# A hybrid decoder layer in float32: the mixer's sixteen group norms, one by one or four together

## The chip, the core and the metric

The kernel runs on one core of a Trainium2 chip. The metric is the device time of one execution in microseconds (us), the median of several runs. The engines are TensorE (PE, matmuls from SBUF into PSUM banks), VectorE (DVE), ScalarE (ACT), GpSimd (POOL) and SyncE (SP, which issues the loads). Each engine works through its own list of instructions in order, and waits where an operand is not there yet.

## What is computed

One layer over 1024 tokens of 1024 features, all in float32, cut to what matters here:

```python
u = rms_norm(x, norm1_g)
z = u @ w_in                      # 3 * 512 convolution columns, 4 * 512 retention columns
# convolution group: 512 features, 8 norm groups of 64
y_conv = cb * causal_dwconv3(cc * ch, conv_w)
y_conv = group_rms_norm(y_conv, conv_norm_g, 8)
# retention group: 4 heads of 128 features, one norm group each
o = chunkwise_retention(q, k, v)
y_ret = group_rms_norm(o, ret_norm_g, 4) * silu(rg)
x = x + concat([y_conv, y_ret]) @ w_out
x = x + relu(rms_norm(x, norm2_g) @ w_up)**2 @ w_down
return rms_norm(x, normf_g)

def group_rms_norm(x, g, n_groups, eps=1e-6):
    xg = x.reshape(shp[:-1] + (n_groups, shp[-1] // n_groups))
    y = xg * rsqrt(mean(xg * xg, axis=-1, keepdims=True) + eps)
    return y.reshape(shp) * g
```

## The kernel before

Features lie on the partitions, tokens on the columns. The unit of side work is a half tile, 128 features by 512 tokens. A float32 product is made of three matmuls of split operands, high by high, low by high and high by low: `wh` and `wl` are a weight's two parts, `uh` and `ul` those of the normed input, `yh` and `yl` those of the mixer's output. The high part is a cast (ACT), the low part a difference (DVE or POOL). Later tiles of the input projection are made in pairs by seven products of 2 x 2 blocks; their operands are `U`, made of `xs`, and each product's bank is combined with others by DVE (`z<-z,b`).

Up to the end of the mixer the products of the input projection fill PE, and everything else goes along with them: retention, convolution, the gate, the norms. That side work is written as generators (`Task`, `spawn`); each `yield` names the engines one of which is to do the next thing, or `None` for a thing that PE does. After each product `tick` calls `background` (line 390), which keeps an estimate of when each engine is through with what it has (`clock`) and of PE's time (`now`), and hands out steps to engines about to be idle. So the written order of every engine comes out of these estimates, and each engine then runs in that order.

The group norms are such generators. The mixer's output has eight tiles, four of the convolution (two norm groups of 64 features each) and four heads (one group of 128), and two halves of tokens: sixteen half tiles, each with a `norm` (line 433) of its own. It squares the half tile on ACT, splits the squares into a high part (ACT) and a low part (DVE or POOL), adds them up over the features of a group by two matmuls with a matrix of ones (`onesr`, or `blkr` with two blocks of 64; lines 445 and 446), which leaves the sum on every partition of a bank of its own; then comes a square root on ACT, a reciprocal on DVE over 128 partitions by 512 columns, and `done`, which scales: heads by `o<-o,r` on POOL or DVE, convolution tiles by `z<-z,sm,r` on DVE, which also multiplies by the norm's weight. At most two norms are open at a time (`asked`, `parts_of_s`). A scaled half tile is split into `yh` and `yl` for the output projection, whose first product takes eight k tiles in the order convolution 0 to 3, heads 0 to 3.

PSUM has eight banks, four for the large products (`pm`) and four for everything else (`pr`).

Of the kernel before, what the change touches and what calls it, by code (L numbers as in the profile page):

```python
# [16 lines left out]
P = 128  # L17
# [7 lines left out]
HB = 512  # hidden features in a block  # L25
# [6 lines left out]
# columns of the packed per-feature vectors  # L32
# [3 lines left out]
# tiles of w_in: 0-11 conv (c, h, b of each), 12-15 q, 16-19 k, 20-23 gate; two heads of q and k  # L36
# are a pair of tiles. The last ones go by pairs.
# [8 lines left out]
class Engine:  # L46
    """An engine, with a rough estimate of when it is through with what it has been given."""
# [23 lines left out]
def hybrid_layer(  # L71
# [12 lines left out]
    zeta: bass.AP,  # L84
    outT: bass.AP,
# [17 lines left out]
    # each engine runs its instructions in the order in which they are written here  # L103
# [24 lines left out]
    # ---- loads of the first phase  # L128
# [38 lines left out]
    plan, parts = [], []  # what makes the next pieces' parts, and the parts that are ready  # L167
# [19 lines left out]
    class Left:  # L187
        """The left operands of the products, for n_ pieces of each of the blocks."""
# [6 lines left out]
        def split(self, n, h=0):  # L195
# [29 lines left out]
    # ---- constants  # L225
    ones = cp.tile([P, 1], F32, name="ones")
    dve.memset(ones, 1.0)
    onesr = xp.tile([P, P], F32R, name="onesr")
    dve.tensor_copy(onesr, ones.to_broadcast([P, P]))
    eps = cp.tile([P, 1], F32, name="eps")  # L230
    dve.memset(eps, EPS)
    act.square(tmp()[:, :1], eps)  # loads the scalar engine's table while the first loads run
    onesf = xp.tile([P, P], F32, name="onesf")
    dve.memset(onesf, 1.0)
    blk = tmp()[:, :P]
    dve.memset(blk, 0.0)
    dve.memset(blk[0:64, 0:64], 1.0)
    dve.memset(blk[64:128, 64:128], 1.0)
    blkr = xp.tile([P, P], F32R, name="blkr")
    dve.tensor_copy(blkr, blk)  # L240
# [3 lines left out]
    def split_scaled(src, g, sl, hi, lo):  # L244
        """hi + lo = src * g, exactly, in two float32r parts."""
        act.activation(hi[:, sl], src[:, sl], AF.Copy, scale=g)
        dve.scalar_tensor_tensor(
            lo[:, sl], src[:, sl], g, f32(hi[:, sl]), ALU.mult, ALU.subtract
        )
# [10 lines left out]
    # ---- first norm's scale and sums  # L260
# [22 lines left out]
    nc.sync.dma_start(zxt, zeta)  # L283
    ropes = [unit(s="rope") for _ in range(6)]
# [3 lines left out]
    def token_rnorms(sums_, r, pool_=pr):  # L288
        """r = 1/sqrt(mean over features + eps), tokens on partitions."""
# [18 lines left out]
    def spread(wide, pool_=pr):  # L308
        """Reciprocal norms, tokens on partitions -> tokens on columns, on every partition."""
# [5 lines left out]
    # ---- v, tokens on partitions, and the tokens' reciprocal norms: on every partition in R,  # L315
    # with tokens on partitions in rtok
# [41 lines left out]

    def mm(piece, banks, rhs, start, stop, ks=range(4)):
        """Adds a piece's product with the parts of 4 tiles of [feature, token] into the banks."""  # L360
# [70 lines left out]
    asked, parts_of_s = [], [0]  # L431

    def norm(y, w, inv_n, done):
        """Norm over groups of features, the sums by a matrix of ones."""
        sq = tmp()
        sh = xp.tile([P, H], F32R, tag="s", name=nm("s"), bufs=4)
        yield (act,)
        act.square(sq, y)
        act.copy(sh, sq)
        eng = yield (dve, pool)  # L440
        slo = xp.tile([P, H], F32R, tag="s", name=nm("s"), bufs=4)
        eng.tensor_sub(slo, sq, f32(sh))
        yield None
        b = bank(pr)
        nc.tensor.matmul(b, w, sh, start=True, stop=False)
        nc.tensor.matmul(b, w, slo, start=False, stop=True)
        now[0] += 0.43
        parts_of_s[0] -= 1
        yield (act,)
        rt = xp.tile([P, H], F32, tag="s", name=nm("r"), bufs=4)  # L450
        act.activation(rt, b, AF.Sqrt, bias=eps, scale=inv_n)
        yield (dve,)
        dve.reciprocal(rt, rt)
        yield from done(rt)
        parts_of_s[0] -= 1

    def norms():
        while asked and parts_of_s[0] <= 2:
            parts_of_s[0] += 2
            y, w, inv_n, done, ready, late = asked.pop(0)  # L460
            spawn(norm(y, w, inv_n, done), ready, late)

    def tick(look=LOOK):
        n = -1
        while n != len(procs):
            n = len(procs)
            background(look)
            norms()

    def split_y_hi(idx, half):  # L470
        """Half a tile of the mixer's output in two parts."""
# [8 lines left out]
    def tile_in(evac):  # L480
        """A tile of the input projection, for both token halves."""
# [46 lines left out]
    def retention(p, q, k):  # L528
        """Step c finishes chunk c - 1 and starts chunk c."""
# [4 lines left out]
        for c in range(NC_ + 1):  # L534
# [30 lines left out]
            if pend is not None:  # L565
# [30 lines left out]
                if pc % 4 == 3:  # L596
                    half = pc // 4
                    for j in range(2):

                        def done(rt, j=j, half=half):  # L600
                            eng = yield (pool, dve)
                            eng.tensor_mul(o[j][:, hs[half]], o[j][:, hs[half]], rt)
                            o_n[h0 + j, half] = o[j]
                            mark(("o", h0 + j, half), eng)

                        asked.append((o[j][:, hs[half]], onesr, 1.0 / P, done, clock[act], 0.0))
# [32 lines left out]
    def conv_b(i, half, z, out, psum):  # L639
# [14 lines left out]
        asked.append((o, blkr, 1.0 / 64, done, clock[eng], LATE * half))  # L654
# [16 lines left out]
    def use(f, half, out, z, psum):  # L671
        """What a quadrant is for."""
# [30 lines left out]
    # ---- tiles of the convolution and of the gate: the first ones as they are, along with the  # L703
    # rest of the retention and the right operands of the seven products; then by pairs
# [25 lines left out]
    def rights(j):  # L730
        """The right operands of the seven products, for a tile of k in each half."""
# [107 lines left out]
    # ---- output projection and residual, by halves of the tokens; then the second norm's  # L839
# [537 lines left out]
```

## Time and profile before

| | |
|---|---|
| median of three runs | 1146.56 us |
| the three runs | 1143.61 to 1148.65 us |
| span of the profiled execution | 1146.0 us |
| mean granted clock of PE, share of full speed | 0.977 |
| PE busy | 1086.0 us, 95% |
| DVE busy | 895.8 us, 78% |
| POOL busy | 606.5 us, 53% |
| ACT busy | 496.3 us, 43% |

Busy is the time in which an engine executes; it says nothing of what the engine was waited for. Idle time of PE is listed with what ended it. Names are the program's, with buffer numbers left out: `z<-z,b` writes `z` from `z` and a bank. Line 65 is that of a helper through which DVE, ACT and POOL are called, so their instructions are told apart by names.

### The profile page before, as it was taken

What the parts mean: (1) busy time and instruction counts of PE and PEld (TensorE: products, weight loads), DVE (VectorE), ACT (ScalarE), POOL (GpSimd) and SP (SyncE); (2) the same over time, 40 slices, a digit from 0 to 9 for tenths busy, and PEclk for the clock granted to TensorE, in tenths of its full rate; (3) what the DMA queues carried; (4) which work ended last, traced back from release to release, by engine and by line L of the source; (5) the groups of instructions that cost most, each with busy time, mean ns of one, the idle gap of its engine ahead of it and who ended that gap; (6) DMA issues with size and microseconds to landing.
All of it is one profiled execution on the core that took longest, in us unless ns stands there. A gap on an engine that the chain in (4) does not pass through costs nothing.

```text
span 1146.0 us, 13780 instructions
## 1 busy us (share of the span) xinstructions
PE 1086.0 (95%) x4880; PEld 887.1 (77%) x4880; DVE 895.8 (78%) x1118; ACT 496.3 (43%) x906; POOL 606.5 (53%) x413
## 2 busy tenths in 40 slices
PE   8999999998798999779999999999999999999897
PEld 6888888886676788657788788787887887887686
DVE  8795686699999647798878788788887887887745
ACT  8212431555344545345444434443434444344553
POOL 6363234457576214877636637437355366374353
PEclk9999999999899999889999999999999999999998
DMA  7311112221112742010120130121211201200104
GB/s 258 138 55 55 28 37 83 79 88 37 37 37 65 274 131 82 0 46 28 56 83 19 55 84 25 58 65 39 73 37 55 83 19 55 83 26 13 55 19 148
DMA packets 40309, 77.73 MB, mean 68 GB/s; under 512 B 4528, under 2 KB 6576, under 8 KB 40240
## 3 DMA queue, kind: packets, MB, share of 16 engines
q1 hardware_dynamic: 40240, 76.85, 21.1%
q8 instruction: 38, 0.62, 0.2%
q14 instruction: 31, 0.25, 0.1%
HBM read 72.64 MB, written 4.19 MB: 67 GB/s over the span
## 4 chain that ended last, share of the span: by engine, by line
PE 50%; DVE 29%; issue 8%; POOL 7%; ACT 5%; DMA 0%; DVEq 0%; POOLq 0%; SPq 0%; ACTq 0%
PE b L365 34%; PE b L1130 8%; DVE wl L65 8%; DVE x L65 7%; PE b L327 4%; POOL t L65 4%; DVE t L65 3%; DVE V L65 2%; ACT wh L65 2%; DVE U L65 2%; ACT t L65 2%; POOL r L65 2%; DVE r L65 1%; DVE z L65 1%; DVE un L65 1%
## 5 line engine op out<-in xcount | busy, mean ns | idle before, releaser
L65 DVE TENSOR_TENSOR wl<-r,wh 128x512 fp32r<-128x512 f32 x273 | 250.4, 924 | 141.1 <-ACT wh L65 140.6
L365 PE MATMUL b<-U,wh 128*128 128x512 f32 x992 | 316.4, 399 | 12.7 <-DVE U L65 8.4
L65 ACT CAST wh<-r 128x512 fp32r<-128x512 f32 x302 | 181.1, 615 | 173.5 <-PE b L365 116.3
L1130 PE MATMUL b<-V,wh 128*128 128x512 f32 x784 | 245.0, 392 | 11.5 <-POOL V L65 10.6
L65 POOL TENSOR_TENSOR r<-r,r 128x512 f32<-128x512 f32 x136 | 205.3, 1515 | 76.9 <-DVE wl L65 36.7
L365 PEld LDWEIGHTS b<-U,wh 128*128 128x128 f32 x992 | 189.9, 192 | 59.5 <-DVE U L65 13.1
L65 DVE TENSOR_TENSOR x<-x,b 128x512 f32<-128x512 f32 (+1 forms) x320 | 197.9, 664 | 11.4 <-PE b L365 11.4
L365 PE MATMUL b<-U,wl 128*128 128x512 f32 x496 | 197.5, 398 | 0.4 <-DVE wl L65 0.4
L65 ACT ACTIVATE t<-t 128x512 f32<-128x512 f32 x128 | 80.8, 632 | 243.3 <-DVE t L65 241.1
L1130 PEld LDWEIGHTS b<-V,wh 128*128 128x128 f32 x784 | 147.7, 188 | 45.6 <-POOL V L65 13.6
L65 POOL TENSOR_TENSOR t<-t,t 128x512 f32<-128x512 f32 x69 | 101.1, 1485 | 124.3 <-ACT t L65 61.9
L1130 PE MATMUL b<-V,wl 128*128 128x512 f32 x392 | 154.4, 394 | 2.4 <-DVE wl L65 2.4
L365 PEld LDWEIGHTS b<-U,wl 128*128 128x128 f32 x496 | 95.0, 192 | 24.2 <-DVE wl L65 4.4
L365 PE MATMUL b<-uh,wh 128*128 128x512 f32 x320 | 107.3, 400 | 4.3 <-DVE z L65 4.3
L65 POOL TENSOR_TENSOR V<-t,V 128x512 fp32r<-128x512 f32 x35 | 51.1, 1459 | 105.1 <-ACT V L65 105.1
L365 PE MATMUL b<-ul,wh 128*128 128x512 f32 x320 | 106.0, 396 | 0.7 <-DVE ul L65 0.7
L365 PE MATMUL b<-uh,wl 128*128 128x512 f32 x320 | 105.6, 395 | 0.0
L65 POOL TENSOR_TENSOR wl<-r,wh 128x512 fp32r<-128x512 f32 x29 | 39.3, 1357 | 98.6 <-ACT wh L65 92.8
L1130 PEld LDWEIGHTS b<-V,wl 128*128 128x128 f32 x392 | 73.8, 188 | 21.3 <-DVE wl L65 6.2
L65 ACT CAST V<-t 128x512 fp32r<-128x512 f32 x98 | 60.4, 617 | 42.9 <-POOL t L65 42.9
L65 DVE TENSOR_TENSOR t<-t,b 128x512 f32<-128x512 f32 x112 | 75.9, 678 | 2.6 <-PE b L365 1.0
L365 PEld LDWEIGHTS b<-uh,wh 128*128 128x128 f32 x320 | 60.2, 191 | 17.5 <-issue 4.4
(157 smaller groups left out, 1511.9 us busy)
## 6 DMA issues: line engine op xcount, KB each, us to landing
r<-w_up_t SPq DMA_DIRECT2D x64, 256.0 KB, 2.6
r<-w_down_t SPq DMA_DIRECT2D x56, 256.0 KB, 2.6
r<-w_in_t SPq DMA_DIRECT2D x48, 256.0 KB, 2.6
r<-w_out_t SPq DMA_DIRECT2D x32, 256.0 KB, 2.7
xt<-xT SPq DMA_DIRECT2D x16, 256.0 KB, 5.4
xs<-xT SPq DMA_DIRECT2D x8, 512.0 KB, 6.2
x<-xT SPq DMA_DIRECT2D x8, 512.0 KB, 7.8
rope<-rope SPq DMA_DIRECT2D x6, 512.0 KB, 7.2
```

The source lines that it names most:

```text
L65: return f(out, *args, **kw)
L327: nc.tensor.matmul(vb[i], a[k][:, tsl], b[k // 2][:, vs], start=(k == 0 and a is uh and b is vh), stop=(k == KT - 1 and a is ul),)
L365: nc.tensor.matmul(b, a[:, k, :], rhs(n, k)[r], start=(start and i == 0), stop=(stop and i == len(ops) - 1),)
L1130: nc.tensor.matmul(b, a, r, start=(i == 0), stop=(i == len(ops) - 1))
```

## The change

The norms go by batches of four half tiles: two heads by two halves, or two convolution tiles by two halves. `ask` collects them; `norms` replaces `norm`.

- Squares and their two parts are made as before. The matmuls that add up the parts now have a selection matrix on the left that has ones in two columns only, so half tile s's sums go to rows 2s and 2s + 1 of one bank that the whole batch shares, and again to rows 32 + 2s and 33 + 2s.
- One square root and one reciprocal over that bank serve the four.
- The result is split: ACT casts it, DVE replaces rows 32 to 63 of the cast by the low part (32x512).
- Each half tile gets its factor back on all partitions by one spread matmul with another selection matrix, into a bank. `done` reads the bank; heads are now scaled by DVE only.
- The selection matrices (128x780) are loaded from DRAM ahead of the rope tables and cast once by ACT; `onesr`, `blkr` and what made them are gone. At most two open norms is no longer a rule.

The rest of the diff takes comments away. Its core:

```diff
+BATCH = 4
+NSELECT = BATCH * P + 2 * (P + 2 * (BATCH - 1))
...
+    sel_raw = unit(s="selw")[:, :NSELECT]
+    nc.sync.dma_start(sel_raw, select)
...
+    sel = unit(F32R, "sel")[:, :NSELECT]
+    act.copy(sel, sel_raw)
...
-    def norm(y, w, inv_n, done):
-        """Norm over groups of features, the sums by a matrix of ones."""
-        sq = tmp()
-        sh = xp.tile([P, H], F32R, tag="s", name=nm("s"), bufs=4)
-        yield (act,)
-        act.square(sq, y)
-        act.copy(sh, sq)
-        eng = yield (dve, pool)
-        slo = xp.tile([P, H], F32R, tag="s", name=nm("s"), bufs=4)
-        eng.tensor_sub(slo, sq, f32(sh))
-        yield None
-        b = bank(pr)
-        nc.tensor.matmul(b, w, sh, start=True, stop=False)
-        nc.tensor.matmul(b, w, slo, start=False, stop=True)
...
+    def norms(kind, items):
+        inv_n = (1.0 / 64, 1.0 / P)[kind]
+        b = None
+        for s, (y, _) in enumerate(items):
+            sq = tmp()
+            sh = xp.tile([P, H], F32R, tag="s", name=nm("s"), bufs=4)
+            yield (act,)
+            act.square(sq, y)
+            act.copy(sh, sq)
+            eng = yield (dve, pool)
+            slo = xp.tile([P, H], F32R, tag="s", name=nm("s"), bufs=4)
+            eng.tensor_sub(slo, sq, f32(sh))
+            yield None
+            if b is None:
+                b = bank(pr)
+            nc.tensor.matmul(b, gather(kind, s), sh, start=(s == 0), stop=False)
+            nc.tensor.matmul(b, gather(kind, s), slo, start=False, stop=(s == len(items) - 1))
+            now[0] += 0.45
         yield (act,)
         rt = xp.tile([P, H], F32, tag="s", name=nm("r"), bufs=4)
         act.activation(rt, b, AF.Sqrt, bias=eps, scale=inv_n)
+        del b
         yield (dve,)
         dve.reciprocal(rt, rt)
-        yield from done(rt)
-        parts_of_s[0] -= 1
...
+        yield (act,)
+        rows = xp.tile([P, H], F32R, tag="s", name=nm("s"), bufs=4)
+        act.copy(rows, rt)
+        yield (dve,)
+        dve.tensor_sub(rows[32:64], rt[32:64], f32(rows[32:64]))
+        for s, (_, done) in enumerate(items):
+            yield None
+            rb = bank(pr)
+            nc.tensor.matmul(rb, place(s), rows, start=True, stop=True)
+            now[0] += 0.23
+            yield from done(rb)
+            del rb
...
                         def done(rt, j=j, half=half):
-                            eng = yield (pool, dve)
-                            eng.tensor_mul(o[j][:, hs[half]], o[j][:, hs[half]], rt)
+                            yield (dve,)
+                            dve.tensor_mul(o[j][:, hs[half]], o[j][:, hs[half]], rt)
```

On DVE, around the last two reciprocals of the convolution tiles before (`z_2428` is tile 3, `r` the factor, `b` a product's bank):

```order
L65 TENSOR_TENSOR z_2599<-z_2599,b_2706 128x512
L65 RECIPROCAL r_2727<-r_2727 128x512
L65 TENSOR_TENSOR z_2600<-z_2600,b_2731 128x512
L65 TENSOR_TENSOR z_2600<-z_2600,b_2653 128x512
L65 TENSOR_TENSOR wl_2773<-r_2595,wh_2772 128x512
L65 TENSOR_TENSOR z_2600<-z_2600,b_2759 128x512
L65 SCALAR_TENSOR_TENSOR z_2428<-z_2428,sm,r_2727 128x512
L65 RECIPROCAL r_2756<-r_2756 128x512
L65 TENSOR_TENSOR wl_2820<-r_2670,wh_2819 128x512
L65 SCALAR_TENSOR_TENSOR z_2428<-z_2428,sm,r_2756 128x512
```

and around the last one after the change, that of tiles 2 and 3 together (`s_2865` holds the rows that the spread matmuls read):

```order
L69 RECIPROCAL r_2835<-r_2835 128x512
L69 TENSOR_TENSOR z_2753<-z_2753,b_2843 128x512
L69 TENSOR_TENSOR z_2752<-z_2753,b_2783 128x512
L69 TENSOR_TENSOR wl_2884<-r_2771,wh_2883 128x512
L69 TENSOR_TENSOR z_2753<-z_2753,b_2868 128x512
L69 TENSOR_TENSOR z_2753<-z_2753,b_2783 128x512
L69 TENSOR_TENSOR s_2865<-r_2835,s_2865 32x512
L69 TENSOR_TENSOR wl_2907<-r_2800,wh_2906 128x512
L69 TENSOR_TENSOR z_2753<-z_2753,b_2891 128x512
```

Two reciprocals with a scaling behind each have become one reciprocal and a 32x512 difference; the scalings stand further on, in the next place.

On PE and on DVE at the end of the mixer. Before, on PE, the last product of the input projection (`uh`, `ul`) is followed by the first output product (`yh_2827` is tile 0):

```order
L365 MATMUL b_2947<-ul_161,wh_2849 128x512
L365 MATMUL b_2947<-uh_153,wl_2850 128x512
L365 MATMUL b_3001<-yh_2827,wh_2884 128x512
L365 MATMUL b_3001<-yl_2828,wh_2884 128x512
L365 MATMUL b_3001<-yh_2827,wl_2885 128x512
L365 MATMUL b_3001<-yh_2831,wh_2884 128x512
```

After, the four spreads stand between them:

```order
L379 MATMUL b_2918<-ul_153,wh_2826 128x512
L379 MATMUL b_2918<-uh_145,wl_2827 128x512
L481 MATMUL b_2938<-s_2865,sel_539 128x512
L481 MATMUL b_2955<-s_2865,sel_539 128x512
L481 MATMUL b_2958<-s_2865,sel_539 128x512
L481 MATMUL b_2961<-s_2865,sel_539 128x512
L379 MATMUL b_2993<-yh_2802,wh_2858 128x512
L379 MATMUL b_2993<-yl_2803,wh_2858 128x512
L379 MATMUL b_2993<-yh_2802,wl_2859 128x512
```

and on DVE, behind the emptying of the last product's bank (the first row), come the scalings of tiles 2 (`z_2199`) and 3 (`z_2392`), in between the gate's products (`o`) and low parts (`yl`):

```order
L69 TENSOR_TENSOR z_2752<-z_2752,b_2918 128x512
L69 SCALAR_TENSOR_TENSOR z_2199<-z_2199,sm,b_2938 128x512
L69 SCALAR_TENSOR_TENSOR o_1568<-z_2753,sm,o_1568 128x512
L69 TENSOR_TENSOR yl_2944<-z_2199,yh_2943 128x512
L69 TENSOR_TENSOR yl_2949<-o_1568,yh_2948 128x512
L69 SCALAR_TENSOR_TENSOR o_1567<-z_2752,sm,o_1567 128x512
L69 SCALAR_TENSOR_TENSOR z_2199<-z_2199,sm,b_2955 128x512
L69 SCALAR_TENSOR_TENSOR z_2392<-z_2392,sm,b_2958 128x512
L69 SCALAR_TENSOR_TENSOR z_2392<-z_2392,sm,b_2961 128x512
L69 TENSOR_TENSOR yl_2965<-z_2392,yh_2964 128x512
```

where before there were these, without any scaling of a convolution tile:

```order
L65 TENSOR_TENSOR z_2782<-z_2782,b_2947 128x512
L65 SCALAR_TENSOR_TENSOR o_1600<-z_2783,sm,o_1600 128x512
L65 TENSOR_TENSOR z_2782<-z_2782,R 128x512
L65 TENSOR_TENSOR yl_2970<-o_1600,yh_2969 128x512
L65 SCALAR_TENSOR_TENSOR o_1599<-z_2782,sm,o_1599 128x512
```

On ACT, the square root of the last batch with what stands behind it (`s_2865` is the cast that waits for DVE's reciprocal, `wh` are casts of weights):

```order
L69 ACT_TABLE_LOAD
L69 ACTIVATE r_2835<-b_2667,eps 128x512
L69 CAST yh_2838<-o_838 128x512
L69 CAST wh_2858<-r_2747 128x512
L69 ACT_TABLE_LOAD
L69 ACTIVATE z_2752<-z_2752 128x512
L69 CAST s_2865<-r_2835 128x512
L69 CAST wh_2883<-r_2771 128x512
L69 CAST wh_2906<-r_2800 128x512
```

Before, no cast of a norm's factor stood among the casts of weights.

## Rows read from the trace of the kernel before

**Rows 1.** The page: busy time of each engine, share of the span, instructions.

```profile
PE 1086.0 (95%) x4880; PEld 887.1 (77%) x4880; DVE 895.8 (78%) x1118; ACT 496.3 (43%) x906; POOL 606.5 (53%) x413
```

**Rows 2.** Windows: stretch, length, busy us (instructions) of PE, PEld, DVE, ACT, POOL; clock.

```profile
60.00:120.00 60.00, 60.00 (x294) 50.65 (x293) 39.67 (x43) 10.77 (x26) 25.74 (x15) 1.00 0.17 53
120.00:240.00 120.00, 120.00 (x635) 102.78 (x634) 87.51 (x102) 45.15 (x101) 45.35 (x33) 1.00 0.22 73
240.40:377.00 136.60, 119.38 (x479) 94.38 (x478) 132.31 (x121) 65.30 (x104) 91.35 (x59) 0.94 0.16 47
377.00:460.00 83.00, 83.00 (x370) 68.79 (x369) 47.74 (x65) 42.31 (x73) 28.09 (x20) 0.98 0.45 155
```

**Rows 3.** Waits of PE from 240 to 380 us: total, times, longest.

```profile
PE b L365 <- DVE z L65: 7.7, 4, 3.6
...
PE b L446 <- POOL s L65: 3.0, 1, 3.0
PE b L446 <- DVE s L65: 2.2, 1, 2.2
```

**Rows 4.** DVE's groups, 240.4 to 377 us: busy, mean ns | idle before.

```profile
L65 DVE RECIPROCAL r<-r 128x512 f32<-128x512 f32 x8 | 26.7, 3342 | 0.7 <-ACT r L65 0.7
L65 DVE TENSOR_TENSOR wl<-r,wh 128x512 fp32r<-128x512 f32 x21 | 21.8, 1038 | 0.2
L65 DVE TENSOR_TENSOR z<-z,b 128x512 f32<-128x512 f32 x28 | 18.9, 674 | 2.7 <-PE b L365 1.9 <-DVE z L65 0.5
...
L65 DVE SCALAR_TENSOR_TENSOR z<-z,sm,r 128x512 f32<-128x512 f32 x6 | 8.0, 1326 | 0.0
...
L65 DVE TENSOR_TENSOR s<-t,s 128x512 fp32r<-128x512 f32 x5 | 6.2, 1238 | 0.0
```

**Rows 5.** Timeline of DVE: start us, duration us, instruction.

```profile
279.13 1.77 DVE L65 TENSOR_TENSOR wl<-r,wh 128x512 fp32r<-128x512 f32 x1
...
294.86 3.34 DVE L65 RECIPROCAL r<-r 128x512 f32<-128x512 f32 x1
...
299.38 0.68 DVE L65 TENSOR_TENSOR wl<-r,wh 128x512 fp32r<-128x512 f32 x1
...
301.19 0.74 DVE L65 SCALAR_TENSOR_TENSOR z<-z,sm,r 128x512 f32<-128x512 f32 x1
```

**Rows 6.** Timeline of PE: start us, duration us, instruction, idle before it.

```profile
298.89 0.77 PE L365 MATMUL b<-uh,wh 128*128 128x512 f32 x1 [3.59 <-DVE z L65]
...
304.15 0.63 PE L365 MATMUL b<-uh,wh 128*128 128x512 f32 x1
304.57 0.47 PE L365 MATMUL b<-ul,wh 128*128 128x512 f32 x1
...
366.31 0.39 PE L365 MATMUL b<-yh,wh 128*128 128x512 f32 x1
366.54 0.39 PE L365 MATMUL b<-yl,wh 128*128 128x512 f32 x1
...
374.40 0.50 PE L365 MATMUL b<-yh,wh 128*128 128x512 f32 x1 [3.17 <-ACT yh L65]
```

**Rows 7.** Windows of 10 us, columns as in rows 2.

```profile
290.00:300.00 10.00, 5.74 (x23) 4.10 (x22) 9.93 (x9) 2.87 (x5) 7.22 (x5) 0.90 0.00 0
300.00:310.00 10.00, 10.00 (x36) 7.96 (x35) 8.03 (x11) 3.81 (x6) 2.98 (x2) 0.76 0.29 80
```

**Rows 8.** Chain that ended last, 240 to 380 us: shares, then start and length.

```profile
by line: PE b L365 30.1%; DVE r L65 9.6%; DVE z L65 9.5%; DVE wl L65 9.0%; DVE xs L65 8.7%; issue 7.9%; DVE cv L65 5.8%; DVE ul L65 4.1%; DVE o L65 4.0%; DVE U L65 3.9%; ACT xs L65 2.8%; DVE yl L65 1.0%; ACT wh L65 0.9%; PE b L446 0.8%; DVE
...
294.94 3.26 DVE r L65
...
298.89 8.24 PE b L365 x23
```

More of the change, by code (lines that the diff above doesn't have):

```diff
@@ L84, in hybrid_layer @@
     zeta: bass.AP,
+    select: bass.AP,
     outT: bass.AP,
@@ L227, in hybrid_layer @@
     dve.memset(ones, 1.0)
-    onesr = xp.tile([P, P], F32R, name="onesr")
-    dve.tensor_copy(onesr, ones.to_broadcast([P, P]))
     eps = cp.tile([P, 1], F32, name="eps")
@@ L234, in hybrid_layer @@
     dve.memset(onesf, 1.0)
[L235 to L240, printed above, removed]
     ident = cp.tile([P, P], F32, name="ident")
@@ L357, in hybrid_layer, with gather, place @@
     prepare(2)
+    sel = unit(F32R, "sel")[:, :NSELECT]
+    act.copy(sel, sel_raw)
+    del sel_raw
+    STRIP = P + 2 * (BATCH - 1)
+    def gather(kind, s):
+        at = BATCH * P + kind * STRIP + 2 * (BATCH - 1 - s)
+        return sel[:, at : at + P]
+    def place(s):
+        return sel[:, s * P : (s + 1) * P]
     def mm(piece, banks, rhs, start, stop, ks=range(4)):
@@ L430, in hybrid_layer @@
     y, y_h, y_l = [None] * KT, [None] * KT, [None] * KT
-    asked, parts_of_s = [], [0]
-    def norm(y, w, inv_n, done):
-        sq = tmp()
-        sh = xp.tile([P, H], F32R, tag="s", name=nm("s"), bufs=4)
-        yield (act,)
-        act.square(sq, y)
-        act.copy(sh, sq)
-        eng = yield (dve, pool)
-        slo = xp.tile([P, H], F32R, tag="s", name=nm("s"), bufs=4)
-        eng.tensor_sub(slo, sq, f32(sh))
-        yield None
-        b = bank(pr)
-        nc.tensor.matmul(b, w, sh, start=True, stop=False)
-        nc.tensor.matmul(b, w, slo, start=False, stop=True)
-        now[0] += 0.43
-        parts_of_s[0] -= 1
+    asked = {}
+    def norms(kind, items):
[16 more added lines that the diff above has]
+            now[0] += 0.45
         yield (act,)
@@ L451, in norm, with ask @@
         act.activation(rt, b, AF.Sqrt, bias=eps, scale=inv_n)
+        del b
         yield (dve,)
         dve.reciprocal(rt, rt)
-        yield from done(rt)
[L455 to L461, printed above, removed]
+        yield (act,)
[10 more added lines that the diff above has]
+            del rb
+    def ask(key, kind, y, done, ready):
+        items = asked.setdefault(key, [])
+        items.append((y, done, ready))
+        if len(items) == BATCH:
+            del asked[key]
+            spawn(norms(kind, [i[:2] for i in items]), max(i[2] for i in items))
     def tick(look=LOOK):
@@ L467, in tick @@
             background(look)
-            norms()
     def split_y_hi(idx, half):
@@ L600, in done @@
                         def done(rt, j=j, half=half):
-                            eng = yield (pool, dve)
-                            eng.tensor_mul(o[j][:, hs[half]], o[j][:, hs[half]], rt)
+                            yield (dve,)
+                            dve.tensor_mul(o[j][:, hs[half]], o[j][:, hs[half]], rt)
                             o_n[h0 + j, half] = o[j]
-                            mark(("o", h0 + j, half), eng)
-                        asked.append((o[j][:, hs[half]], onesr, 1.0 / P, done, clock[act], 0.0))
+                            mark(("o", h0 + j, half), dve)
+                        ask(("heads", p), 1, o[j][:, hs[half]], done, clock[act])
             pend = new
@@ L652, in done @@
             mark(("y", i, half), dve)
-        asked.append((o, blkr, 1.0 / 64, done, clock[eng], LATE * half))
+        ask(("conv", i // 2), 0, o, done, clock[eng])
     def gate(h, half, z, g, psum):
@@ L1300, in _constants @@
     zeta = np.exp(lg[None, :] * (P - 1.0 - i)[:, None]) * scale
-    return [np.ascontiguousarray(a, np.float32) for a in (rope, decay, zeta)]
+    place = np.zeros((P, BATCH, P))
+    strips = np.zeros((P, 2, P + 2 * (BATCH - 1)))
+    c = 2 * (BATCH - 1)
+    for at in (0, 32):
+        for g in range(2):
+            for s in range(BATCH):
+                place[at + 2 * s + g, s, g * 64 : (g + 1) * 64] = 1.0
+            strips[g * 64 : (g + 1) * 64, 0, at + c + g] = 1.0
+            strips[:, 1, at + c + g] = 1.0
+    select = np.concatenate([place.reshape(P, -1), strips.reshape(P, -1)], axis=1)
+    return [np.ascontiguousarray(a, np.float32) for a in (rope, decay, zeta, select)]
 def kernel(x, norm1_g, w_in, conv_w, conv_norm_g, ret_norm_g, w_out, norm2_g, w_up, w_down,
@@ L1346 @@
     )
-    rope, decay, zeta = _constants()
+    rope, decay, zeta, select = _constants()
     arrays = {
@@ L1362 @@
         "zeta": zeta,
+        "select": select,
     }
```

## The prediction

> **What bounds the kernel now.** The table of engines comes first: TensorE (PE) is busy 95% of the span and VectorE (DVE) 78% [rows 1]. Neither is the answer everywhere, so the second view cuts the span where the changed work lies. The kernel up to the end of the mixer has 16 group norms. From 120 to 240 us PE has no idle time at all, from 377 to 460 us again none; between, from 240.4 us (the second convolution tile's product leaves its bank) to 377.0 us (the first output tile is added to x), DVE is busy 132.3 of 136.6 us and PE 119.4 [rows 2]. There DVE is the bound, and there eight of the sixteen norms' reciprocals run.
>
> The third view says who PE waits for in that stretch: 7.7 us for DVE's combining of two banks (`z`), 5.3 us at two sum matmuls for the low part `s` of the squares, made by POOL and by DVE [rows 3]; most of the rest of PE's 17 us is the 3.17 us at 374.40 for a head's `yh` [rows 6]. The fourth groups DVE's instructions: a reciprocal takes 3.34 us, five times a two-operand instruction's 0.67 [rows 4]. The timeline shows one acting: from 294.86 to 298.12 us DVE is in a reciprocal, the bank that PE needs is emptied behind it, and PE, after 3.59 us of idling, goes on at 298.89 [rows 5, 6, 8]. Until 304.57 it issues a matmul each 0.427 us, at full clock each 0.227 us [rows 6]; the granted clock of that slice and the next is 0.90 and 0.76, a mixture of 2.4 and 1.2 GHz [rows 7]. The chain of work that ended last takes both pieces in, the reciprocal and the slow products [rows 8].
>
> **The change, part by part.**
>
> *Reciprocals and square roots.* The instruction order has four reciprocals where there were sixteen, in the bound stretch three where there were eight: 5 x 3.34 = 16.7 us of DVE saved. The twelve square roots less lie on ACT, busy 65 of 136.6 us [rows 2]: nothing.
>
> *What DVE gets for it.* In the stretch the order shows DVE with 120 instructions before and 133 after. Gone besides the reciprocals: six `z<-z,sm,r`, two `wl`, one `xs` difference. New: eight `z<-z,sm,b` (the factor now read from PSUM), four `o<-o,b` (two were POOL's, two belonged to heads scaled earlier), three low parts of 32x512, four `s`, two each of `z<-z,R`, `z<-z,cv` and `yl`, two sums of squares: 27. No row shows `z<-z,sm,b`; it is bounded below by `z<-z,b`, one operand in PSUM, 0.674 us, and above by `z<-z,sm,r`, 1.326 us in the mean and 0.74 us alone [rows 4, 5]; I take 0.72, because the operand from PSUM is what it has in common with the first and the scalar with the second. The 32x512 low part is bounded by 0.68 and 1.77 us, the same operation on 128 partitions alone and with POOL beside it [rows 5]. With every instruction at its price alone: gone 16.7 + 6 x 0.74 + 3 x 0.68 = 23.2; new 8 x 0.72 + 19 x 0.68 = 18.7; net -4.5 us.
>
> *How much of it is lengthening.* A `wl` took 1.77 us at 279.13, while POOL ran, and 0.68 us at 299.38 [rows 5]. Reciprocals and the instructions that read a bank are never lengthened (3.342 and 0.674 in the mean [rows 4]). So 8 x 3.34 + 33 x 0.67 = 48.8 us of the stretch are cover under which POOL costs DVE nothing; the other 80 instructions take 132.3 - 48.8 = 83.5 us, 29 us more than 80 x 0.68. With 59 POOL instructions in the stretch [rows 2] that is 0.49 us each, or 0.77 for each that falls outside the cover (48.8 of 136.6, 36%). After the change POOL has 51 there by the order (`o<-o,r`, some `s` and `z<-z,cv` go to DVE), and the cover is 3 x 3.34 + 45 x 0.67 = 40 us, 31% of some 130. 51 x 0.77 x 0.69 = 27 us: another -1.9. DVE's term is **-6.4 us**. Ends: if every added instruction costs its group's mean (1.238 for `s`, 0.674 for what reads a bank [rows 4]), the sum shrinks to about -2.5; if the lengthening goes with POOL's instructions alone, at 0.49 each, it is -4.5 - 3.9 = -8.4.
>
> The rule that speaks against this edit is in the Trainium skill, "SBUF — State Buffer", section "Who interferes with whom": a DVE instruction with two SBUF inputs contends with a GpSimd instruction that reads SBUF, one with at most one SBUF input does not. The trace agrees (1.77 against 0.68 us; the reciprocal always 3.34), so the change takes away DVE instructions of the kind that does not contend. By it DVE's term is the -6.4 above; without it the -8.4, and the time 1138.6.
> A second one, "VectorE: DVE Perf Modes", section "The TRN2 errata", gives a VectorE instruction with PSUM 62 cycles more than one with SBUF alone; by it the twelve that now read PSUM would cost an estimated 0.8 us more, 1141.4 in all. The rows differ: 0.674 with a bank, 0.68 without [rows 4, 5].
>
> *PE's waits and clock.* The clock's part of the stall behind the reciprocal at 294.86 us lies on the chain: 13 matmuls at 0.427 instead of 0.227 us are **-2.6 us** if that stall goes [rows 6, 8]. The wait itself is DVE's time and is in DVE's term. What is late next there is the next emptying, since DVE stays full.
>
> *Matmuls.* 32 sum matmuls become 32 gathers and 16 spreads. Ahead of 240 us there are four fewer, at 0.227 us on a full PE [rows 2, 6]: **-0.9 us**. In the stretch there are twenty more, 4.5 us, under PE's 17 us of idling: nothing, unless DVE ceases to bind.
>
> *New places where PE waits.* Gathers and spreads stand in PE's order at some 23 places of the stretch instead of 7. Of the seven, two waited, 5.3 us together [rows 3]; but in the chain of waits second sum matmuls (line 446) hold only 0.8% of the 140 us from 240 to 380, 1.1 us [rows 8]. At 1.1/7 each sixteen more cost 2.5 us, at 5.3/7 each 12 us. I take half of the lower, **+1.2 us**, since what they wait for is made by engines that have less to do.
>
> *The end of the mixer.* The second convolution batch is finished last. Its four spreads stand directly ahead of the first output product, and the scaling of tiles 2 and 3 behind the last emptying on DVE. The output product needs tile 3 as the fourth of eight k tiles: 15 of its 24 matmuls follow what comes last, before it was 3 (three `yh`/`yl` sets of head 3 at 374.40 us [rows 6]). 12 x 0.227 = **+2.7 us**. The scalings themselves are in DVE's term.
>
> *Small parts.* The selection matrix's load stands ahead of the rope loads on SP's queue and its cast on ACT ahead of the first products; PE is full from 60 to 240 us [rows 2], so a rope tile that comes a microsecond later is hidden by products; uncovered it would be that microsecond. Constants dropped at the start ran while DVE waited for loads: nothing. The MLP's instructions are in the same order on every engine.
>
> Sum: -6.4 - 2.6 - 0.9 + 1.2 + 2.7 = -6.0 us. The profiled execution spans 1146.0 us; the median of the three times is 1146.56, so the sum is put against the median: **1140.6 us**.
>
> **Rivals.**
> *PE becomes the bound.* If DVE is relieved so that PE seldom waits, the stretch is PE's: 479 + 20 matmuls x 0.227 = 113 us, plus the end's wait of 3 and some 5 for half clock and gaps, 121.5 instead of 136.6: 1131 us. For it: DVE's waits are nearly all of PE's. Against: DVE alone has 132 us there and loses a few only.
> *No gain.* The work swapped for reciprocals is two-operand work at its mean price: -2.5, the tail +2.7, places +2.5, the rest -0.9 and the clock's 2.6 not given back: about +2: 1146 to 1148. For it: `s` at 1.24 and `wl` at 1.04 in the mean; against: eight POOL instructions less.
> *Slower: ACT held behind the batch.* The cast of the reciprocal's rows stands in ACT's order ahead of casts of weights (`wh`) and waits for the reciprocal on DVE, which waits for four half tiles' sums. In the written order weights are cast two to three products ahead, each product 12 x 0.227 = 2.7 us, so 5 to 8 us of lateness are covered. Beyond that PE stops: each batch then costs a stall like the 3.59 us and the 2.6 us of half clock behind it, three batches 18.6 us, against the 6 gained: 1159 us; with one or two batches 1147 to 1153. It decides from the point where the reciprocal starts more than 8 us after the square root. For it: DVE has no slack; against: ACT is half idle.
> That the change would not do what it says, the order excludes: the reciprocals are gone.
>
> **How the numbers follow.** The sum, with DVE's ends and the places' doubled, runs from 1136 to 1145, chance 0.45, and a little over half of that lies beyond 0.5% faster. PE the bound: 0.18. No gain: 0.25. ACT held: 0.12. Half a per cent, 5.7 us, is about what a measurement of this kernel can tell from no change; the bounds are 1140.8 and 1152.3. Faster: 0.26 + 0.18 and a little of the no-gain case, 0.46; same 0.43; slower 0.11. The range leaves out half of the slower case and the outer part of PE's: 1131 to 1150.
>
> **What would show it.** In the changed trace: three reciprocals between the second convolution tile's product and the first output tile; that stretch at 130 to 131 us with DVE still 95% busy or more; POOL's lengthening of two-operand instructions unchanged; a granted clock above 0.94 in it; a PE wait at the first output product on tile 2 or 3 rather than on head 3; `z<-z,sm,b` at 0.70 to 0.75 us. DVE below 93% with PE full would make the first rival right; ACT idle ahead of a cast `s<-r` with PE waiting for `wh` or `wl`, the third; a stretch of 136 us with two-operand instructions at 1.1 us and more, the second. A stall of PE of over 3 us at the four spreads would make the end's term wrong.

## The result

The changed kernel takes 1149.28 us in the median of 14 runs, beside 1146.28 us of the kernel before on the same chip: a ratio of 1.0027, 95% interval 1.0015 to 1.0040, 3 us slower. Two repeats of it on other chips gave 1.0041 (1.0026 to 1.0056) and 1.0036 (1.0023 to 1.0050). The forecast was 1140.6 us, so the range of 1131 to 1150 holds the time, but the sign is wrong: it went the other way, by half of what was forecast.

The page of the changed kernel shows what was meant to happen. DVE's busy time fell by 35.5 us, POOL's by 23 [rows 1]:

```profile
span 1147.5 us, 13774 instructions
## 1 busy us (share of the span) xinstructions
PE 1085.9 (95%) x4896; PEld 884.5 (77%) x4896; DVE 860.3 (75%) x1119; ACT 490.6 (43%) x899; POOL 583.1 (51%) x399
```

Where the time went is read by cutting both profiles at the same events: the second convolution tile's product (where the stretch of [rows 2] begins), the last product of the input projection, the first output tile's addition `x<-x,b`, and the eighth. First the kernel before, then the change (stretch, length, busy us and instructions of PE, PEld, DVE, ACT, POOL; granted clock, DMA):

```profile
240.47:366.31 125.84, 112.02 (x449) 88.84 (x448) 121.72 (x107) 60.47 (x96) 87.93 (x57) 0.93 0.13 38
366.31:376.98 10.67, 7.28 (x30) 5.45 (x29) 10.57 (x15) 4.76 (x8) 3.42 (x2) 0.97 0.46 153
376.98:416.72 39.74, 39.74 (x171) 32.73 (x170) 20.28 (x29) 20.69 (x36) 11.18 (x8) 0.96 0.66 236
```

```profile
240.66:359.93 119.27, 110.56 (x465) 87.27 (x464) 108.07 (x117) 62.29 (x101) 73.84 (x49) 0.99 0.14 42
359.93:380.48 20.55, 11.77 (x35) 7.99 (x35) 14.58 (x17) 6.01 (x10) 5.66 (x4) 0.75 0.65 243
380.48:418.59 38.11, 38.11 (x170) 31.56 (x169) 20.65 (x29) 20.61 (x36) 11.20 (x8) 1.00 0.49 152
```

The last input product comes 6.6 us earlier than before, with PE's clock at 0.99 instead of 0.93. From there to the first addition it takes 20.55 us instead of 10.67, 9.9 more, of which the next stretch returns 1.6 (its clock is full, that of before was not yet). In this pair of profiles the start differs by 0.2 us and the rest by -0.4, which makes the 1.5 us between the two spans. The medians are 3 us apart. The profile of the change is of a run at its median (1149.25 us), that of the kernel before is a long one: its span is 1146.0 us, where later runs of the same kernel have 1144.7 to 1145.8 in the median. In runs 8 and 10 below, which leave this part of the kernel before as it is, it takes 124.7 us to the last product, not 125.84. Against these the gain up to there is 5.5 us rather than 6.6. A stall early in the kernel, which this profile of the change doesn't have, comes on top in some runs; it is told below.

At the end of the mixer PE and DVE of the changed kernel read (start us, duration us, instruction, idle before it):

```profile
359.93 1.17 PE L481 MATMUL b<-s,sel 128*128 128x512 f32 x4
...
362.10 0.40 PE L379 MATMUL b<-yh,wl 128*128 128x512 f32 x1
368.06 0.80 PE L379 MATMUL b<-yh,wh 128*128 128x512 f32 x1 [5.56 <-ACT yh L69]
...
373.30 0.79 PE L379 MATMUL b<-yh,wh 128*128 128x512 f32 x1 [2.83 <-ACT yh L69]
```

```profile
366.02 0.67 DVE L69 TENSOR_TENSOR z<-z,b 128x512 f32<-128x512 f32 x1
366.62 0.73 DVE L69 SCALAR_TENSOR_TENSOR z<-z,sm,b 128x512 f32<-128x512 f32 x1
367.27 1.31 DVE L69 SCALAR_TENSOR_TENSOR o<-z,sm,o 128x512 f32<-128x512 f32 x1
368.51 0.68 DVE L69 TENSOR_TENSOR yl<-z,yh 128x512 fp32r<-128x512 f32 x1
369.27 0.69 DVE L69 TENSOR_TENSOR yl<-o,yh 128x512 fp32r<-128x512 f32 x1
369.88 0.74 DVE L69 SCALAR_TENSOR_TENSOR o<-z,sm,o 128x512 f32<-128x512 f32 x1
370.54 2.06 DVE L69 SCALAR_TENSOR_TENSOR z<-z,sm,b 128x512 f32<-128x512 f32 x3
373.28 0.69 DVE L69 TENSOR_TENSOR yl<-z,yh 128x512 fp32r<-128x512 f32 x1 [0.68 <-ACT yh L69]
```

The spreads run at 359.93 without a wait; six output matmuls later PE stands, first for tile 2's `yh`, then for tile 3's. DVE empties the last input bank at 366.02, 6.1 us behind the product, and only then scales tiles 2 and 3: the low part that PE needs for tile 3 comes at 373.28. The kernel before has the same lag and a short way behind it, from the last emptying to the last low part 2.0 us instead of 7.3:

```profile
372.36 0.67 DVE L65 TENSOR_TENSOR z<-z,b 128x512 f32<-128x512 f32 x1
...
374.38 0.69 DVE L65 TENSOR_TENSOR yl<-o,yh 128x512 fp32r<-128x512 f32 x1
```

So the 9.9 us are 5.2 us between the last emptying and the last low part, and 4.6 us behind it: 7.2 us to the first addition instead of 2.6, because 14 of 24 matmuls are left rather than two, and PE issues them each 0.43 us up to 378.0 us, at the lower clock, before it is back at 0.23 (0.75 is the mean of the stretch).

The rows that answer to [rows 3] and [rows 4], PE's waits from the start to 400 us and DVE's groups from 240.6 to 359.9 us:

```profile
PE b L379 <- ACT yh L69: 8.4, 2, 5.6
...
PE b L465 <- DVE s L69: 5.2, 5, 2.4
PE b L465 <- POOL s L69: 2.2, 2, 1.6
...
PE b L481 <- DVE s L69: 0.6, 1, 0.6
PE b L464 <- ACT s L69: 0.5, 1, 0.5
```

```profile
L69 DVE TENSOR_TENSOR wl<-r,wh 128x512 fp32r<-128x512 f32 x16 | 18.6, 1161 | 2.8 <-ACT wh L69 2.8
...
L69 DVE RECIPROCAL r<-r 128x512 f32<-128x512 f32 x3 | 10.0, 3340 | 0.0
L69 DVE TENSOR_TENSOR s<-t,s 128x512 fp32r<-128x512 f32 x9 | 8.3, 921 | 0.3 <-ACT s L69 0.3
L69 DVE SCALAR_TENSOR_TENSOR z<-z,sm,b 128x512 f32<-128x512 f32 x4 | 2.9, 736 | 0.0
L69 DVE TENSOR_TENSOR s<-r,s 32x512 fp32r<-32x512 f32 x3 | 2.8, 927 | 0.1
```

PE waits for `z` no more. It waits for `s` at the gathers, 7.4 us for low parts instead of 5.3 and 0.5 for a high part, 0.6 us at a spread (L481), and for `yh`.

### The profile page after: what moved, and what is told of

Same layout as the page of the kernel before. It is cut to its first block, busy times and chain, and to the rows that moved or that the text cites. A ratio compares the mean times of both kernels' runs of the same rounds, so it can differ in the third digit from the quotient of the medians.

```text
span 1147.5 us, 13774 instructions
## 1 busy us (share of the span) xinstructions
PE 1085.9 (95%) x4896; PEld 884.5 (77%) x4896; DVE 860.3 (75%) x1119; ACT 490.6 (43%) x899; POOL 583.1 (51%) x399
## 4 chain that ended last, share of the span: by engine, by line
PE 28%; DVE 23%; issue 7%; POOL 7%; ACT 4%; DVEq 0%; POOLq 0%; ACTq 0%
PE b L379 19%; PE b L1159 8%; DVE x L69 7%; DVE wl L69 7%; POOL t L69 4%; DVE t L69 3%; DVE V L69 2%; ACT wh L69 2%; POOL r L69 2%; ACT t L69 2%; DVE U L69 2%; DVE un L69 1%; POOL V L69 1%; PE b L293 1%; POOL x L69 0%
## 5 line engine op out<-in xcount | busy, mean ns | idle before, releaser
L1159 PE MATMUL b<-V,wh 128*128 128x512 f32 x784 | 245.3, 392 | 11.6 <-POOL V L69 10.7
L1159 PEld LDWEIGHTS b<-V,wh 128*128 128x128 f32 x784 | 147.7, 189 | 45.6 <-POOL V L69 13.7
L69 POOL TENSOR_TENSOR wl<-r,wh 128x512 fp32r<-128x512 f32 x32 | 44.8, 1404 | 116.3 <-ACT wh L69 104.7
L379 PEld LDWEIGHTS b<-ul,wh 128*128 128x128 f32 x320 | 60.5, 189 | 13.4 <-DVE ul L69 0.4
```

Source lines behind the costliest of these rows:

```text
L69: return f(out, *args, **kw)
L379: nc.tensor.matmul(b, a[:, k, :], rhs(n, k)[r], start=(start and i == 0), stop=(stop and i == len(ops) - 1),)
L1159: nc.tensor.matmul(b, a, r, start=(i == 0), stop=(i == len(ops) - 1))
```

## The experiments

Theory A: the gain is there up to the last input product and is given back at the end of the mixer, where the last batch finishes. Theory B: it is used up all along, by PE's waits at gathers and spreads and by two-operand work. The first four runs were made on one chip. The stages of all profiles (the start, then the lengths to the last input product, the first and the eighth addition, and the rest; us):

| kernel | start | to last product | to 1st addition | to 8th | rest | span |
|---|---|---|---|---|---|---|
| before | 240.47 | 125.84 | 10.67 | 39.74 | 729.28 | 1146.0 |
| the change | 240.66 | 119.27 | 20.55 | 38.11 | 728.91 | 1147.5 |
| 1, last four apart | 244.57 | 124.38 | 10.86 | 40.43 | 729.26 | 1149.5 |
| 2, first half first | 244.05 | 119.26 | 18.84 | 38.09 | 728.56 | 1148.8 |
| 3, last by tile | 244.28 | 123.26 | 10.30 | 36.83 | 727.63 | 1142.3 |
| 4, five short | 240.90 | 118.10 | 10.66 | 39.72 | 729.02 | 1138.4 |
| 5, the change again | 241.24 | 119.19 | 19.56 | 38.08 | 728.13 | 1146.2 |
| 6, the change, zr later | 240.41 | 119.19 | 21.15 | 38.09 | 729.96 | 1148.8 |
| 7, last by tile, zr later | 240.53 | 124.10 | 10.19 | 36.94 | 727.64 | 1139.4 |
| 8, before, tie forced | 246.98 | 124.72 | 10.67 | 39.73 | 729.10 | 1151.2 |
| 9, the change, tie forced | 246.65 | 119.93 | 21.00 | 38.09 | 726.13 | 1151.8 |
| 10, before, zr later | 240.24 | 124.69 | 10.67 | 39.75 | 729.15 | 1144.5 |
| 11, the change a third time | 244.39 | 119.08 | 19.70 | 38.10 | 729.23 | 1150.5 |

In all five profiles with the change's order the last product comes after 119.1 to 119.9 us and the first addition 19.6 to 21.2 us behind it; in the three with the order of the kernel before it is 124.7 to 125.8 and 10.7. So the gain and the loss are no accident of one execution.

**1. The last four norms apart.**

```diff
...
     def ask(key, kind, y, done, ready):
+        if key == ("conv", 1):
+            w = (blkr, None)[kind]
+            alone.append((y, w, (1.0 / 64, 1.0 / P)[kind], done, ready))
+            return
         items = asked.setdefault(key, [])
...
```

(`norm` of the kernel before comes back for these four.)

> Three batches as in the change; the four half tiles of convolution tiles 2 and 3 have a norm each as before (two blocks of ones, own bank, own reciprocal), so six reciprocals instead of four. Theory A (the gain is there and is given back behind the last input product, because the last batch is finished there): the last input product ends 5 to 6 us earlier than before, and from it to the first output tile's addition it takes 10 to 12 us as before, not 20.5; time 1140 to 1142, faster than before by 4 to 6 us. Theory B (what DVE gains is taken by waits of PE at gathers and spreads and by two-operand work all along the stretch, so undoing one batch only adds reciprocals): 1149 or more.

Measured: 1150.06 us, 1.0029 (1.0016 to 1.0042) to before: the time is theory B's. The end of the mixer is back at 10.86 us, as theory A says, but the last product comes only 1.5 us earlier than before. A new wait stands there, at a sum matmul of one of the four single norms:

```profile
PE b L504 <- POOL s L69: 4.3, 1, 4.3
```

The estimates that hand out the steps wrote everything around these norms anew, so this run shows that the end can be had back, not that the gain stays. Its start at 244.57 us, 4.1 us late, was in neither theory; without it the span would be about that of before.

**2. The first token half first.**

```diff
...
-        for s, (_, done) in enumerate(items):
+        for s, (_, done, _) in sorted(enumerate(items), key=lambda e: e[1][2]):
...
```

(The third element is the token half.)

> The change with the order of the last steps altered: of each batch the two half tiles of the first token half are spread and scaled first. In the written order tile 3's first half is then behind one scaling less... in numbers: two scalings of 0.66 us and no more move behind it. Theory A: the second wait of PE at the first output product gets 1.3 to 2 us shorter, time 1147 to 1148, between the change and before. Theory B: no difference from the change, 1149.

Measured: 1150.77 us, 1.0041 (1.0025 to 1.0057). Up to the last product two scalings of tiles 0 and 1, with their spreads, have changed places and nothing else, and the two profiles agree to 0.01 us from the start to there. The end is 18.84 us instead of 20.55, 1.7 us for two scalings less ahead of tile 3; PE's second wait is 1.52 us instead of 2.83, at the lower end of what theory A expected. The time did not follow, because the start is 3.4 us late in this run, with the instructions of the change ahead of it.

**3. Tiles 2 and 3 as batches of two.**

```diff
...
+    SAME = (("heads", 0), ("heads", 1), ("conv", 0))
...
-        if len(items) == BATCH:
+        if len(items) == (BATCH if key in SAME else 2):
...
-        ask(("conv", i // 2), 0, o, done, clock[eng], half)
+        ask(("conv", i // 2 if i < 2 else i), 0, o, done, clock[eng], half)
...
```

> As the kernel with the first token half first, but tiles 2 and 3 of the convolution are batches of their own, two half tiles each: five reciprocals, and in the written order tile 3's scalings stand a whole product and more ahead of the last input product. Theory A: no wait of PE at the first output product for a convolution tile; last input product 6 us earlier than before, time 1139 to 1141, the fastest of these. Theory B: 1148 to 1150.

Measured: 1145.79 us, 0.9993 (0.9981 to 1.0005): neither theory's time. In stages theory A holds at the end, which takes 10.30 us with no wait of PE for a convolution tile, and from the start to the eighth addition it is 170.4 us, 5.9 less than before and 7.5 less than the change. (The first addition waits 1.17 us for the load of `x` there, so the border of these two stages lies late.) But the last product is 2.6 us earlier than before, not 6: with one more reciprocal, and tile 3's scalings now ahead of it, DVE has more to do up to there (113.4 us, the change 108.1). And again the start is late, 244.28.

**4. Five short reciprocals in the kernel before.**

```diff
...
-        dve.reciprocal(rt, rt)
+        n_rec[0] += 1
+        if n_rec[0] in (10, 11, 13, 14, 15):
+            clock[dve] = max(clock[dve], now[0]) + dve.cost(H, "reciprocal")
+            nc.vector.reciprocal(rt[:, :32], rt[:, :32])
+        else:
+            dve.reciprocal(rt, rt)
```

(The estimate in `clock` goes on as for a whole reciprocal, so every engine keeps its written order.)

> The kernel before in its own written order; five of the eight reciprocals in the bound stretch work on 32 of their 512 columns, the rest of the factor stays the square root (part of the computation is left out). It takes 5 x 3 = 15 us off DVE there and adds nothing anywhere. Theory A (DVE bounds the stretch and a reciprocal is worth nearly its time): DVE busy in the stretch 117 instead of 132 us, the stretch 8 to 12 us shorter until PE binds, time 1135 to 1139. Theory B (reciprocals are cover that costs little, since POOL's work then lengthens other instructions): 1143 or more, DVE's two-operand instructions longer in the mean.

Measured: 1140.51 us, 0.9953 (0.9935 to 0.9970). From the start to the first addition 128.76 us instead of 136.51, 7.8 less; DVE busy there 120.4 instead of 132.3. The time lies between the two theories, 1.5 us above A's range and 2.5 below B's. The five take 0.34 us each, 15.0 us less than whole ones, and took 11.9 us off DVE, since two-operand work got longer where they had been:

```profile
L65 DVE TENSOR_TENSOR wl<-r,wh 128x512 fp32r<-128x512 f32 x21 | 23.9, 1138 | 4.8 <-ACT wh L65 4.6
...
L456 DVE RECIPROCAL r<-r 128x32 f32<-128x32 f32 x5 | 1.7, 344 | 0.7 <-ACT r L65 0.7
```

`wl` was 1.038 us in the mean before [rows 4]. A microsecond of reciprocal was worth half a microsecond of time, and a microsecond off DVE's busy time (7.8 for 11.9) two thirds.

**The late start.** In runs 1 to 3 PE waits at 67 to 68 us for a weight's low part, where the kernel before and the first profile of the change do not. Theory C: two instructions of DVE and POOL start so close to each other there that either can be first. Theory D: the late starts belong to those three kernels. Four runs on a second chip, then three on a third.

**5. The change again, unaltered.**

> The change itself, unaltered, for a second look. Theory C (a tie: at 65 us a 128x1024 product of the rope tables on POOL and the first of four low parts on DVE start within 30 ns of each other; if POOL is first DVE is held 2.3 us, PE waits some 2 us for that low part and runs a few us at the lower clock; either outcome can come in any run): the profile shows either start, the second convolution tile's product at 240.7 or at 244.3 us, and the time is 1148 to 1151. Theory D (the three slower starts came with those kernels' other edits): 240.7 again, 1149.

Measured: 1151.13 us, 1.0041; in its profile the start is 241.24 and there is no stall. That profiled run, 1149.18 us, is the lowest of the eight.

**6. zr behind the low parts, in the change.**

```diff
-                for h in range(NH):
-                    dve.tensor_scalar_mul(zr[:, h, :], rtok, zxt[:, h : h + 1])
...
     prepare(2)
+    for h in range(NH):
+        dve.tensor_scalar_mul(zr[:, h, :], rtok, zxt[:, h : h + 1])
```

> The change with one thing moved: the four small products of zr on DVE (128x8, needed by the retention only) stand behind the two low parts that PE needs at 65 us instead of ahead of them. Theory C: PE has no wait at 67 us in any run, the second convolution tile's product comes at 240.5 us, and the time is that of the change less 3.7 us times the share of runs in which the tie was lost: 1146 to 1149. Theory D: the time of the change, 1149.

Measured: 1148.65 us, 1.0025 (1.0013 to 1.0037), 2.5 us below the change on the same chip; start 240.41. As theory C has it, though the two ratios' intervals overlap. With no tie to lose the change is still 0.25% slower than the kernel before.

**7. The third run's kernel with the same move.**

> Batches by convolution tile at the end and the first token half first, as in the third run, with zr moved as above. Theory C: start at 240.5 instead of 244.3 us, the rest as in the third run: 1146 - 5.9 - 1 = 1139 to 1141, faster than both kernels. Theory D: as the third run, 1145 to 1146.

Measured: 1142.24 us, 0.9965 (0.9954 to 0.9975), faster than both kernels by 4 us and more, though 1 to 3 us short of what was expected. The start is 240.53, and the scalings of tile 3 stand at 352 and 358 us, ahead of the last product at 364.63; PE's wait for head 3's `yh` is 0.58 us, where it was 3.17 before [rows 6]:

```profile
352.14 0.74 DVE L69 SCALAR_TENSOR_TENSOR z<-z,sm,b 128x512 f32<-128x512 f32 x1
...
358.45 0.73 DVE L69 SCALAR_TENSOR_TENSOR z<-z,sm,b 128x512 f32<-128x512 f32 x1
...
370.13 0.49 PE L379 MATMUL b<-yh,wh 128*128 128x512 f32 x1 [0.58 <-ACT yh L69]
```

Up to the eighth addition it is 5.0 us ahead of the kernel before. Of these 1.7 us lie ahead of the last product, and against the 124.7 us of runs 8 and 10 only 0.6; 3.3 us lie behind it. A further 1.6 us is in the rest, and its cause was not looked for. So little of this run's gain is the saving on DVE that the batches were made for. The written order at the end is new, and no run tells how much of the 3.3 us is due to the batches of two.

**8. The tie forced, in the kernel before.**

```diff
+    for h in range(1):
+        dve.tensor_scalar_mul(zr[:, h, :], rtok, zxt[:, h : h + 1])
     prepare(2)
```

> The kernel before with one 128x8 product of zr repeated on DVE ahead of the low parts, under 0.1 us of work, so that POOL's last rope product is first at 65 us. Theory C: PE waits about 2 us at 67 us for a low part and runs below full clock behind it, the second convolution tile's product comes at 244 us, and the time is 3 to 4 us above before: 1149.5 to 1150.5. Theory D: no change, 1146.5.

Measured: 1149.86 us, 1.0030 (1.0018 to 1.0042), as theory C expected of the time. The edit makes more than a lost tie: the repeated product is itself held beside POOL's (2.41 us), so the first low part starts only at 67.78 us and is held too (2.46 us). In the profile, the slowest of the twelve runs with 1153.01 us, PE waits 3.79 us, twice what it waits in run 11, and the stretch starts at 246.98 instead of 244. So the run shows that a late low part costs time, not what the tie alone costs.

**9. The same edit, in the change.**

> The change with one 128x8 product of zr repeated on DVE ahead of the low parts, as in the eighth run for the kernel before: POOL is first at 65 us in every run. Theory C: PE waits at 67 to 70 us, the second convolution tile's product at 244 us or later, time 3 to 4 us above the change with zr moved (1148.65): 1151.7 to 1152.7; if the change itself lies near this, it mostly loses the tie. Theory D: 1149 to 1150.

Measured: 1153.58 us, 1.0052 (1.0039 to 1.0064), 0.9 us above theory C's range; start 246.65, with the same wait of 3.79 us as in run 8.

**10. zr behind the low parts, in the kernel before.**

> The kernel before with the four small products of zr behind the two low parts that PE needs at 65 us. If the kernel before wins the tie nearly always, its time stays within 0.7 us: 1146 to 1147. If it loses it in a third of its runs, 1145 to 1145.5.

Measured: 1146.25 us, 0.9997 (0.9984 to 1.0009): the kernel before gains nothing that can be measured by taking the tie out. The interval reaches down to 1.8 us less, half of what a lost tie costs in run 11, so the run doesn't show how seldom that kernel loses it. (The edit is that of run 6.)

**11. The change a third time.**

> The change itself a third time, on the same chip as the two above. Theory C: between 1148.6 (tie won in all runs) and the time of the kernel with the tie lost, and the profile shows a start at 240.7 to 241.3 or at 244 us. Theory D: 1149 with 240.7.

Measured: 1152.61 us, 1.0036 (1.0023 to 1.0050). This profile of the unaltered change has the stall: start 244.39, span 1150.5. The same kernel starts either way, so the late start does not belong to the edits of runs 1 to 3: theory D is out. The timelines of DVE, POOL and PE around 65 us, first in the first profile of the change, then in the third:

```profile
65.01 0.68 DVE L69 TENSOR_TENSOR wl<-r,wh 128x512 fp32r<-128x512 f32 x1
...
65.02 2.93 POOL L69 TENSOR_TENSOR rope<-rope,R 128x1024 f32<-128x1024 f32 x1
```

```profile
64.95 2.92 DVE L69 TENSOR_TENSOR wl<-r,wh 128x512 fp32r<-128x512 f32 x1
...
64.92 2.41 POOL L69 TENSOR_TENSOR rope<-rope,R 128x1024 f32<-128x1024 f32 x1
...
67.92 0.74 PE L379 MATMUL b<-uh,wl 128*128 128x512 f32 x2 [1.94 <-DVE wl L69]
```

In the first DVE makes the low part in 0.68 us, and POOL's product takes 2.93. In the third the low part takes 2.92 us and POOL's product 2.41; PE waits 1.94 us and runs below full clock for some microseconds (0.86 from 70 to 80 us), and the stretch starts 3.7 us later. The starts fit theory C in these two profiles, DVE 10 ns ahead and 30 ns behind. They don't in run 1, where DVE starts 20 ns ahead and is held all the same:

```profile
65.09 2.91 DVE L69 TENSOR_TENSOR wl<-r,wh 128x512 fp32r<-128x512 f32 x1
...
65.11 2.34 POOL L69 TENSOR_TENSOR rope<-rope,R 128x1024 f32<-128x1024 f32 x1
```

So what decides between the two is open; the order of the starts in a profile does not tell it. How often the change loses the tie when it is only timed no profile shows. Its three ratios average 1.0035; with the tie taken out it was 1.0025, and the stall's 3.7 us are 0.0032, so an estimate from these is about a third of the runs, with intervals as wide as that. Whether the change loses it more often than the kernel before is not shown.

## Why the prediction was wrong

**The step that failed is the end of the mixer**, put at +2.7 us: 9.9 us to the first addition, 8.3 to the eighth. I counted the matmuls behind the last low part, 12 more at full clock, and left out the rest with the sentence that the scalings are in DVE's term. That holds only while DVE bounds the whole stretch to its end. It did not: up to the last product DVE was busy 108.1 of 119.3 us, and the scalings of the last batch fell behind the last emptying, where nothing but DVE and ACT could go on. There 5.2 us came on the path, and the matmuls left over ran partly at the lower clock, 4.6 us instead of the 2.7. Four more profiles of the change's order have the same loss, 8.9 to 10.5 us to the first addition. The sign that I named, a stall of over 3 us at the spreads, came six matmuls behind them: 5.56 us, at tile 2.

**DVE's term and the clock** were right as a sum: -6.4, -2.6 and +1.2 for the new waits make -7.8 to the last product; measured -6.6, and -5.5 against runs 8 and 10. Their parts were not. DVE's work in the whole stretch, to the first addition, fell by 9.6 us (122.65 busy in 139.82, 88% and not the 95% that I named), beyond the end of -8.4 that I gave. By the prediction's own division the 85 instructions outside the cover are lengthened by 24.7 us, 4.4 less than before instead of 1.9; the other 5.2 us are prices, put at 4.5. But in run 4 a microsecond off DVE's busy time is worth two thirds of one, and here 13.7 us less of it up to the last product gave 6.6, so the time should not have been put equal to DVE's sum. The stall behind a reciprocal and its half clock went as forecast (clock 0.93 to 0.99).

**The new places** cost more than the +1.2 taken: 7.9 us of waits for `s` at the gathers against 5.3 [rows 3], and 0.6 at a spread, 3.2 us together. PE's waits for `z`, 7.7 us before, went to nil in exchange.

**Prices of single instructions** held: `z<-z,sm,b` 0.736 us against the 0.72 taken, the 32x512 part 0.93 between its bounds. The Trainium skill, "VectorE: DVE Perf Modes", section "The TRN2 errata", would have the first 62 cycles longer than the form from SBUF; that took 0.74 alone [rows 5], so the trace shows no such difference.

**The small parts** hid a term. "PE is full from 60 to 240 us" was true of the profile that I read, and rests on the low part at 64.58 us not being held (0.68 us in that profile). -0.9 us was expected up to 240. Measured was 0.2 us more than before with the tie won, where two short waits that are new, 0.6 us at a spread and 0.4 for `vl`, took up the matmuls' part, and 3.9 us more with it lost.

**The rivals.** The slower one, ACT held behind the row cast, is not what happened: that cast waited 0.46 us at the last batch, and PE waited for `wh` once, 0.8 us. "No gain" came near the time (1146 to 1148) by a different mechanism, spread along the stretch; the stages show most of the gain there at the last product. PE did not become the bound.

## What to carry to other kernels

Work gathered into a batch is finished with its last member. Ask where the batch's results stand in each engine's order against the last thing that the next phase waits for: the saving is counted over a stretch, the loss falls on its end. Here a kernel with smaller batches at the end, and with the tie taken out, came to 1142.24 us, 0.35% below the kernel before; most of that lies behind the last product, so it is a better end more than a kept saving.

A term summed over an engine's busy time is worth its full amount only while that engine stays full; in run 4 it was two thirds. One run that takes away only that work tells the rate.

## What the runs showed of the hardware

Identical code ran either way from one execution to the next, and the difference was 3.7 us up to the start of the stretch. POOL's 128x1024 product holds up a DVE instruction that runs into it (2.92 us instead of 0.68 in the third profile of the change), and DVE's instruction holds POOL's likewise (2.93 instead of 2.41 in the first). The Trainium skill, "SBUF — State Buffer", section "Who interferes with whom", says that whoever issues first has the shared ports for its whole instruction and the other waits, there of DVE's two-port modes; these traces show the holding for a two-operand instruction from SBUF, too. Who issued first they do not resolve: in run 1 DVE starts 20 ns ahead by the profile and is the one held.

The prediction told held instructions from others by the number of their inputs from SBUF. That does not cover all: the 128x8 products of `zr`, with one input tile and a column of factors, end with POOL's products beside them, three of the four after 2.43 us each in the first profile of the change. That is far from their size: a reciprocal of 128x4 takes 0.18 us in the mean in the profile of the kernel before.
